# Hybrid mLSTM / stick-breaking layer: k projected ahead of q in the first set of heads, and all its heads turned by VectorE and transfers

## The chip, the cores and the metric

The kernel runs on one core of one Trainium2 chip. The metric is the device time of one execution in microseconds (us); lower is better. A core has a matrix engine (TensorE, PE in the profile, with its weight loads listed as PEld), a vector engine (VectorE, DVE), a scalar engine (ScalarE, ACT) and GpSimd (POOL). Transfers are issued from the queue of an engine; most of this kernel's are issued from SyncE (SP). Each engine works through its own instructions in the order in which the program issued them, and waits for the others by semaphores.

## The reference

One layer over x of 512 tokens by 1024 channels, all in float32. After an RMS norm, one input projection `w_in` gives the inputs of two token mixers and of the merge gates. Mixer A is an mLSTM with 4 heads of width 256. Mixer B, where the change lies, is stick-breaking attention with 8 heads of width 128:

```python
qs = rmsnorm(to_heads(sq, SB_HEADS), sb_q_norm_w)
ks_ = rmsnorm(to_heads(sk, SB_HEADS), sb_k_norm_w)
...
    z = jnp.einsum('bhtd,bhsd->bhts', qb, kb).astype(jnp.float32) * scale
...
    log_beta = jax.nn.log_sigmoid(z)
    log_1mb = jnp.where(causal, jax.nn.log_sigmoid(-z), 0.0)
    between = lax.cumsum(log_1mb, axis=3, reverse=True) - log_1mb
    a = jnp.where(causal, jnp.exp(log_beta + between), 0.0)
    outs.append(jnp.einsum('bhts,bhsd->bhtd', a.astype(v.dtype), vb))
```

Both mixers' outputs are gated, projected, merged by sigmoid gates and projected once more, and x is added.

## The kernel before

**Products in three parts.** To keep float32 accuracy every operand is split into a high half (a copy on ACT in a format that PE multiplies fast, `split` at L96, L97) and a low half (the difference, on DVE, L98), and each product is three matmuls: high by high, high by low, low by high (`mm3`, L91 to L94; the second of the three reads the low half of the moving operand). The split of a weight block writes `wh` and `wl`.

**Units.** All dense work is a list `units` of 512 KB weight blocks. A unit is 24 matmuls of 512 columns. The list is in the order of L862 to L1136. With the first set of four attention heads (`sets[0]`) it begins: four units for q (0 to 3), four for k (4 to 7), four for v (8 to 11), four for the gate z (12 to 15); then the second set's q (16 to 19), k (20 to 23) and so on. q, k and v are token groups: their four units go through the contraction, and each unit adds to all four PSUM banks (`dps`, four in all), one for each block of 128 tokens; they are evacuated together after the fourth unit. The very first group is different (`first`, L164): there each unit is one block of 128 tokens, so that the blocks are evacuated one by one, after units 0, 1, 2 and 3. z is a channel group: each unit fills one bank, evacuated a step later (L348, L350).

**The main loop** (L1263) makes one pass, here called a step, for each unit c. In this order it issues: the evacuation of unit c-1; the functions that are due at c (`later`, filled by `defer(n, fn)` with n steps of delay); the splits of units up to c+2 and loads further ahead (`ahead`); the first half of unit c's matmuls; one stage of each attention or mLSTM head in progress (`act`; in the steps of `REST`, among them 11 and 16, none moves on); the first stage of a head that starts now (`pend`, with `SB_START` at L27); the second half of unit c's matmuls.

**q and k of a head.** `qk_group` (L355) adds the bias to each token block (L364), squares and sums on ACT (L373), and takes the power -1/2 on POOL (L274, L275; for q a negative copy follows, L378). k is scaled by that on DVE a step later (L386); q isn't, its factor is applied in the sigmoids (L478, L482). Attention needs q and k with channels on partitions, so raw q and k must be turned. There are two ways. Either PE transposes the four blocks of a head through an identity into a PSUM bank (L455), when the head starts. Or `turn` (L399) does it for two heads at a time: four DVE transposes of 32 by 32 blocks (L405); a step later 16 transfers that put the blocks in place (`move`, L408 to L415), into a tile `tz`; for q, two more steps later, a DVE scaling with the norm weights (`weight`, L417 to L419). `TURNED` (L30) lists what takes the second way, as (name, set, pair of heads); in the first set all of q and the second pair of k. For k of the first pair PE does it.

**A head** (`head`, L444) is a generator. Its first stage splits the turned q and k into `qtt` and `ktt`. The next two hold the scores (L470), the sigmoids on ACT, the masks on POOL, the scan along the keys on DVE (L486) and products (L487), and DVE transposes of the weights (L504). Later stages move those blocks by transfers (L522) and multiply with v.

**The order before around the change.** q is evacuated in steps 1 to 4 and turned at steps 5 and 7 (moves at 6 and 8, weightings at 8 and 10). k is evacuated at step 8, scaled at 9 and 10, and its second pair turned at 11 with the move at 12. Heads 0, 1, 2, 3 start at steps 10, 13, 16, 20; heads 0 and 1 with four PE transposes each. All 16 transfers of a move go on SP's queue in the first set; in the second set every other one goes on POOL's (L414).

Of the kernel before, what the change touches and what calls it, by code (L numbers as in the profile page):

```python
# [17 lines left out]
TB = 4  # L18
# [3 lines left out]
C_SQ, C_SK, C_SV, C_SZ, C_GM, C_GS = 5128, 6152, 7176, 8200, 9224, 10248  # L22
# [1 line left out]

SB_START = [10, 13, 16, 20, 26, 28, 32, 34]  # L27
M_START = [52, 56, 70, 76]
GATES_PREP, GATES_START, GATES_SCAN = 2, 4, 35
TURNED = {("q", 0, 0), ("q", 0, 1), ("q", 1, 0), ("q", 1, 1), ("k", 0, 1), ("k", 1, 1)}  # L30
REST = {11, 16, 20, 23, 24, 32, 44, 64}
AHEAD, LOADS = 2, 4

# [2 lines left out]
def tile_hybrid_layer(  # L36
# [16 lines left out]
    nc = tc.nc  # L53
# [21 lines left out]
    def blk(tag, dt=F32, shape=(512,), name=None, p=128):  # L75

        where = mp if tag in MISC else sp
        return where.tile([p] + list(shape), dt, name=name or tag, tag=tag, bufs=BUFS[tag])

    def two(tag, dt=F32, name=None):  # L80

        t = blk(tag, dt, (2, 512), name=name)
        return t[:, 0, :], t[:, 1, :]

    def dense_ps():
        return psd.tile([128, 512], F32, name="dps", tag="dps")
# [4 lines left out]
    def mm3(ps, ah, al, bh, bl, first, last):  # L91
        nc.tensor.matmul(ps, ah, bh, start=first, stop=False)  # L92
        nc.tensor.matmul(ps, ah, bl, start=False, stop=False)  # L93
        nc.tensor.matmul(ps, al, bh, start=False, stop=last)  # L94
# [53 lines left out]
    def tok_group(src, c0, sta, evac, first=False, b0=None, row=None):  # L148
        ps = [None] * TB
        n0 = len(units)  # L150

        def evacs(ps):
            rest = None
            for tb in range(TB):
                then = evac(tb, ps[tb])
                if rest:
                    rest()
                rest = then
            if rest:
                rest()  # L160

        if row is not None:
            later.setdefault(n0 + (0 if first else 2), []).append(lambda: row.append(bias_row(b0)))
        if first:  # L164
            for tb in range(TB):
                u = Unit(src, c0, 256 * tb)
                u.evac = lambda tb=tb: evac(tb, f_ps[tb])
                units.append(u)
            return
        for g in range(4):  # L170
            u = Unit(src, c0, 256 * g)

            def mm(half, u=u, g=g):
                for tb in (2 * half, 2 * half + 1):
                    if g == 0:
                        ps[tb] = dense_ps()
                    for i in range(2):
                        k = 2 * g + i
                        sh, sl = sta(k, tb)
                        mm3(ps[tb], sh, sl, u.wh[:, i, :], u.wl[:, i, :], k == 0, k == KT - 1)  # L180

            u.mm = mm
            u.heavy = g == 3
            u.evac = (lambda: evacs(ps)) if g == 3 else (lambda: None)
            units.append(u)
# [11 lines left out]
    def defer(n, fn):  # L197
        later.setdefault(now[0] + n, []).append(fn)
# [74 lines left out]
    def rstd(dst, ssq, n, eps):  # L273
        nc.gpsimd.tensor_scalar(dst, ssq, 1.0 / n, eps, op0=OP.mult, op1=OP.add)  # L274
        nc.gpsimd.tensor_tensor(dst, dst, mhalf[:, 0:dst.shape[1]], op=OP.pow)  # L275
# [50 lines left out]
    def bias_row(c0):  # L326
        b = blk("brow")
        nc.sync.dma_start(b, bass.AP(tensor=b_in.tensor, offset=b_in.offset + c0, ap=[[0, 128], [1, 512]]))
        return b
# [6 lines left out]
    class SbSet:  # L336
# [18 lines left out]
        def qk_group(self, name, c0):  # L355
            row = []

            half = []

            def evac(tb, ps):  # L360
                if tb % 2 == 0:
                    half.extend(two("qk", name=name + "raw"))
                t = half[tb]
                nc.vector.tensor_tensor(t, ps, row[0], op=OP.add)  # L364
                self.raw[name].append(t)

                def norm():
                    ssq = tiny.tile([128, 4], F32, name="ssq", bufs=2)
                    rr = tiny.tile([128, 8], F32, name="r" + name, bufs=8 if name == "q" else 4)
                    r = rr[:, 0:4]  # L370
                    junk = blk("acc", BF, (128,), name="sqj")
                    for h in range(4):
                        nc.scalar.activation(junk, t[:, h * 128:(h + 1) * 128], AF.Square,  # L373
                                             accum_out=ssq[:, h:h + 1])
                    rstd(r, ssq, 128, EPS)
                    if name == "q":
                        rn = rr[:, 4:8]
                        nc.gpsimd.tensor_scalar(rn, r, -1.0, None, op0=OP.mult)  # L378
                        self.r.append((r, rn))
                        if tb == TB - 1:  # L380
                            defer(1, lambda: self.turn(name, 0))
                    else:
                        def scale():
                            for h in range(4):
                                hs = slice(h * 128, (h + 1) * 128)
                                nc.vector.tensor_scalar(t[:, hs], t[:, hs], r[:, h:h + 1], None, op0=OP.mult)  # L386
                            if tb == TB - 1:
                                done.add(("k", self.s))
                                defer(1, lambda: self.turn(name, 1))
                        defer(1, scale)  # L390

                if tb < 2 or name == "q" and self.s == 0:
                    norm()
                else:
                    defer(1, norm)

            tok_group(w_in, c0 + 512 * self.s, h_sta, evac, name == "q" and self.s == 0, c0 + 512 * self.s, row)

        def turn(self, name, g):  # L399

            ty = sp.tile([128, 8, TB, 32], F32, name="ty", tag="A", bufs=4)
            for tb in range(TB):
                nc.vector.transpose(ty[:, :, tb, :],  # L405
                                    self.raw[name][tb][:, 256 * g:256 * g + 256].rearrange("p (x j) -> p x j", j=32))

            def move():  # L408
                tz = blk("qk", F32, (2, 4, 128), name="tz")
                self.tz[name, g] = tz  # L410
                src = ty.rearrange("p (h b) i j -> p b h (i j)", h=2)
                for b in range(4):
                    for a in range(4):
                        q = nc.gpsimd if self.s and a % 2 else nc.sync  # L414
                        q.dma_start(tz[32 * b:32 * b + 32, :, a, :], src[32 * a:32 * a + 32, b])  # L415

            def weight():  # L417
                z = self.tz[name, g]
                nc.vector.tensor_scalar(z, z, qkw, None, op0=OP.mult)  # L419

            defer(1, move)
            if name == "q":
                defer(3, weight)
            if name == "q" and g == 0:
                defer(2, lambda: self.turn(name, 1))
# [18 lines left out]
        def head(self, h):  # L444
            hs = slice(h * 128, (h + 1) * 128)
            tr = []
            for name in ("q", "k"):
                th, tl = own = two("qk", FR, name=name + "tt")
                if (name, self.s, h // 2) in TURNED:
                    tp = self.tz[name, h // 2][:, h % 2].rearrange("p a (i j) -> p i a j", j=32)  # L450
                    th, tl = [x.rearrange("p (i a j) -> p i a j", a=4, j=32) for x in own]
                else:
                    tp = att_ps()
                    for tb in range(TB):
                        nc.tensor.transpose(tp[:, tb * 128:(tb + 1) * 128], self.raw[name][tb][:, hs], ident)  # L455
                if name == "q" and not (name, self.s, h // 2) in TURNED:
                    nc.scalar.activation(th, tp, AF.Copy, scale=qkw)
# [403 lines left out]

    sets = [SbSet(0), SbSet(1)]  # L862
    pairs = [MPair(0), MPair(1)]
    sets[0].qk_group("q", C_SQ)
    sets[0].qk_group("k", C_SK)
    sets[0].v_group()
    sets[0].z_group()
    sets[1].qk_group("q", C_SQ)
# [362 lines left out]
    for s in (0, 1):  # L1231
        for h in range(4):
            pend.append((SB_START[4 * s + h], 1,
                         lambda s=s: ("k", s) in done, lambda s=s, h=h: sets[s].head(h)))
# [102 lines left out]
```

## Time and profile before

| | us |
|---|---|
| median of 3 runs | 689.77 |
| range of the 3 runs | 689.24 to 689.87 |
| the profiled execution, whole | 689.49 |
| its span, from the first to the last instruction | 687.8 |
| PE busy in it | 681.0 |
| DVE busy | 467.2 |
| ACT busy | 337.1 |
| POOL busy | 111.7 |

The profile is of one execution. A row of its timeline has the start and the length in us, the engine, the line of the kernel, the operation, what it writes and reads, and how often; in brackets the idle time of the engine before it and what ended that. PE's matmuls overlap, so their rows last longer than the distance between their starts, and it is the starts that tell how fast PE goes. A row of the waits has who waited, for whom, us in total, times, and the longest.

### The profile page before, as it was taken

How to read it: one execution, taken by the hardware profiler on the slowest of the kernel's cores; microseconds unless marked ns; L12 is line 12 of the kernel's file. 1: busy time of each engine (PE TensorE's matmuls, PEld its weight loads, DVE VectorE, ACT ScalarE, POOL GpSimd, SP SyncE). 2: the span in 40 equal slices, each digit the busy share in tenths (PEclk: the TensorE clock that was granted, in tenths of full speed). 3: DMA queues.
4: the chain of work that ended last, by engine and by line, in shares of the span. 5: the costliest groups of instructions: out<-in, count | busy, mean ns of one | idle time of the engine just before them, and what ended most of it. 6: DMA issues, size and time to landing. Idle time of an engine off the chain costs nothing.

```text
span 687.8 us, 9389 instructions
## 1 busy us (share of the span) xinstructions
PE 681.0 (99%) x3162; PEld 568.9 (83%) x3162; DVE 467.2 (68%) x819; ACT 337.1 (49%) x631; POOL 111.7 (16%) x266
## 2 busy tenths in 40 slices
PE   8999999999999999999999999999999999999997
PEld 5888888888888888888888888888888888888876
DVE  6746787777997886789834648994352364445997
ACT  6245465566455653344466533448554343344451
POOL 4122042365430310000001210000112000111020
PEclk9999999999999999999999999999999999999999
DMA  7433543435463533643341343434223456599333
GB/s 250 139 95 107 160 138 105 134 112 149 134 171 86 124 111 83 139 95 92 107 117 53 107 109 85 128 91 134 68 64 90 115 176 200 141 206 205 121 82 103
DMA packets 122289, 84.74 MB, mean 123 GB/s; under 512 B 19018, under 2 KB 105956, under 8 KB 122240
## 3 DMA queue, kind: packets, MB, share of 16 engines
q1 hardware_dynamic: 119600, 77.97, 40.3%
q0 software_dynamic: 2496, 6.03, 4.7%
q8 instruction: 25, 0.41, 0.2%
q14 instruction: 24, 0.20, 0.1%
q10 hardware_dynamic: 144, 0.13, 0.1%
HBM read 66.22 MB, written 2.15 MB: 99 GB/s over the span
## 4 chain that ended last, share of the span: by engine, by line
PE 98%; DVE 1%; DMA 1%; SPq 0%; issue 0%; ACT 0%
PE dps L92 28%; PE dps L93 27%; PE dps L94 27%; PE aps L93 3%; PE aps L94 3%; PE aps L92 3%; PE dps L1216 1%; PE dps L1217 1%; PE dps L1218 1%; PE aps L811 1%; PE aps L813 1%; PE aps L812 1%; DMA stg<-in_w_in_dram 1%; PE aps L305 0%; DVE hl L317 0%; PE aps L591 0%
## 5 line engine op out<-in xcount | busy, mean ns | idle before, releaser
L98 DVE TENSOR_TENSOR wl<-stg,wh 128x1024 fp32r<-128x1024 f32 x92 | 112.5, 1223 | 106.0 <-ACT wh L97 105.5
L92 PE MATMUL dps<-hh,wh 128*128 128x512 f32 x448 | 175.0, 391 | 0.0
L94 PE MATMUL dps<-hh,wl 128*128 128x512 f32 x448 | 174.4, 389 | 0.0
L93 PE MATMUL dps<-hl,wh 128*128 128x512 f32 x448 | 174.4, 389 | 0.0
L97 ACT ACTIVATE wh<-stg 128x1024 fp32r<-128x1024 f32 x92 | 96.8, 1052 | 64.5 <-PE dps L94 44.3
L94 PEld LDWEIGHTS dps<-hh,wl 128*128 128x128 f32 x448 | 84.1, 188 | 17.7
L93 PEld LDWEIGHTS dps<-hl,wh 128*128 128x128 f32 x448 | 84.2, 188 | 16.8
L92 PEld LDWEIGHTS dps<-hh,wh 128*128 128x128 f32 x448 | 84.1, 188 | 16.7
L92 PE MATMUL dps<-wh,hh 128*128 128x512 f32 x224 | 87.7, 392 | 0.0
L94 PE MATMUL dps<-wh,hl 128*128 128x512 f32 x224 | 87.3, 390 | 0.0
L93 PE MATMUL dps<-wl,hh 128*128 128x512 f32 x224 | 87.2, 389 | 0.0
L94 PEld LDWEIGHTS dps<-wh,hl 128*128 128x128 f32 x224 | 42.0, 188 | 9.0
L92 PEld LDWEIGHTS dps<-wh,hh 128*128 128x128 f32 x224 | 42.1, 188 | 8.3
L93 PEld LDWEIGHTS dps<-wl,hh 128*128 128x128 f32 x224 | 42.1, 188 | 8.2
L704 DVE SCALAR_TENSOR_TENSOR acc<-tmp,vec,acc 128x511 f32<-128x511 f32 (+2 forms) x48 | 36.0, 750 | 1.7
L707 ACT ACTIVATE tmp<-acc 128x512 f32<-128x512 f32 x16 | 10.1, 633 | 50.8 <-DVE acc L704 50.8
L480 POOL TENSOR_SCALAR_AFFINE_SELECT om<-om 128x128 f32<-128x128 f32 x32 | 15.3, 479 | 96.2 <-ACT om L478 96.1
L486 DVE TENSOR_TENSOR_SCAN om<-om 128x512 f32<-128x512 f32 (+3 forms) x32 | 26.7, 834 | 5.5 <-POOL om L480 5.5
L764 POOL TENSOR_SCALAR_AFFINE_SELECT w_all<-om 128x128 f32<-128x128 f32 x16 | 5.3, 363 | 144.4 <-DMA om<-rb_d 144.4
L478 ACT ACTIVATE om<-aps,rq 128x512 f32<-128x512 f32 (+3 forms) x32 | 16.8, 524 | 21.0 <-PE aps L94 21.0
L94 PE MATMUL dps<-yh,wl 128*128 128x512 f32 x64 | 24.9, 389 | 0.0
L92 PE MATMUL dps<-yh,wh 128*128 128x512 f32 x64 | 24.9, 389 | 0.0
(249 smaller groups left out, 1217.8 us busy)
## 6 DMA issues: line engine op xcount, KB each, us to landing
stg<-in_w_in_dram SPq DMA_DIRECT2D x87, 512.0 KB, 3.9
az<-ay SPq DMA_DIRECT2D x128, 40.0 KB, 2.9
stg<-in_w_proj_s_dram SPq DMA_DIRECT2D x8, 512.0 KB, 4.7
B<-in_w_out_dram SPq DMA_DIRECT2D x8, 512.0 KB, 6.6
stg<-in_w_proj_m_dram SPq DMA_DIRECT2D x8, 512.0 KB, 5.9
wl<-stg POOLq DMA_DIRECT2D x8, 512.0 KB, 5.9
tz<-ty SPq DMA_DIRECT2D x72, 32.0 KB, 1.9
brow<-in_b_in_dram SPq DMA_DIRECT2D x8, 256.0 KB, 4.5
```

The source lines that it names most:

```text
L92: nc.tensor.matmul(ps, ah, bh, start=first, stop=False)
L93: nc.tensor.matmul(ps, ah, bl, start=False, stop=False)
L94: nc.tensor.matmul(ps, al, bh, start=False, stop=last)
L97: nc.scalar.activation(hi, src, AF.Copy)
L98: nc.vector.tensor_tensor(lo, src, hi.bitcast(F32), op=OP.subtract)
L478: nc.scalar.activation(om[:, 0:n], zp, AF.Sigmoid, scale=rn[:, h:h + 1])
L480: nc.gpsimd.affine_select(out=om[:, ts], in_=om[:, ts], compare_op=OP.is_gt, fill=1.0, base=0, channel_multiplier=1, pattern=[[-1, 128]])
L486: nc.vector.tensor_tensor_scan(back, back, back, 1.0, op0=OP.mult, op1=OP.bypass)
L704: nc.vector.scalar_tensor_tensor(acc[:, j:], t[:, 0:T - j], cw(3 - j, ch), acc[:, j:], op0=OP.mult, op1=OP.add)
L707: nc.scalar.activation(t, acc, AF.Sigmoid)
L811: nc.tensor.matmul(nm[:, 0:258], ph, vh, start=j == 0, stop=False)
L812: nc.tensor.matmul(sum_v, ph, vl, start=False, stop=False)
```

## The change

Line numbers of the kernel before apply. In the first set:

- k's group is issued ahead of q's, so k takes the place of the first group (units 0 to 3, block by block) and q that of the second (units 4 to 7, evacuated together).
- k's first pair joins `TURNED`: heads 0 and 1 no longer have PE transposes. k's scale is due a step after each evacuation (steps 2 to 5); its first pair is turned at step 6, its second at 7, with moves at 7 and 8.
- q is turned at the end of its evacuation: the first pair at step 8 (move at 9, weighting at 11), the second at step 10 (move at 11, weighting at 13).
- In the second set q's first turn is due at the same step as before, only put down at another place.
- The moves of the first set send every other transfer on POOL's queue, as those of the second set do.
- Head 0 starts at step 11 rather than 10, head 2 at 15 rather than 16. Steps 11 and 16 are in `REST`, so the stages after the first stay in the steps that they had.

```diff
-SB_START = [10, 13, 16, 20, 26, 28, 32, 34]
+SB_START = [11, 13, 15, 20, 26, 28, 32, 34]
...
-TURNED = {("q", 0, 0), ("q", 0, 1), ("q", 1, 0), ("q", 1, 1), ("k", 0, 1), ("k", 1, 1)}
+TURNED = {("q", 0, 0), ("q", 0, 1), ("q", 1, 0), ("q", 1, 1), ("k", 0, 0), ("k", 0, 1), ("k", 1, 1)}
...
                         self.r.append((r, rn))
-                        if tb == TB - 1:
-                            defer(1, lambda: self.turn(name, 0))
                     else:
...
                             if tb == TB - 1:
                                 done.add(("k", self.s))
-                                defer(1, lambda: self.turn(name, 1))
+                                if self.s == 0:
+                                    defer(1, lambda: self.turn(name, 0))
+                                defer(2 - self.s, lambda: self.turn(name, 1))
                         defer(1, scale)
 
-                if tb < 2 or name == "q" and self.s == 0:
+                if name == "q" and tb == TB - 1:
+
+                    if self.s:
+                        defer(2, lambda: self.turn(name, 0))
+                    else:
+                        self.turn(name, 0)
+                if tb < 2 or name == "k" and self.s == 0:
                     norm()
                 else:
                     defer(1, norm)
 
-            tok_group(w_in, c0 + 512 * self.s, h_sta, evac, name == "q" and self.s == 0, c0 + 512 * self.s, row)
+            tok_group(w_in, c0 + 512 * self.s, h_sta, evac, name == "k" and self.s == 0, c0 + 512 * self.s, row)
...
-                        q = nc.gpsimd if self.s and a % 2 else nc.sync
+                        q = nc.gpsimd if a % 2 else nc.sync
...
+    sets[0].qk_group("k", C_SK)
     sets[0].qk_group("q", C_SQ)
-    sets[0].qk_group("k", C_SK)
```

## The prediction

> **What bounds the kernel now.** I read the page first: its first two parts and the chain that ended last.
>
> ```profile
> span 687.8 us, 9389 instructions
> PE 681.0 (99%) x3162; PEld 568.9 (83%) x3162; DVE 467.2 (68%) x819; ACT 337.1 (49%) x631; POOL 111.7 (16%) x266
> PEclk9999999999999999999999999999999999999999
> PE 98%; DVE 1%; DMA 1%; SPq 0%; issue 0%; ACT 0%
> ```
>
> TensorE (PE) is busy for 99% of the span at full granted clock, and 98% of the chain that sets the end is its own work. Next I asked who PE waits for:
>
> ```profile
> PE dps L1184 <- DVE idle L1179: 1.5, 1, 1.5
> PE dps L1216 <- DVE hh L309: 1.0, 1, 1.0
> PE aps L305 <- DVE x L297: 0.8, 2, 0.6
> ```
>
> That is the whole list: 3.3 us, all before 14 us. Later PE never waits. So two things alone can move the end: PE instructions that go away, and a new wait on PE. A relieved queue or engine is worth nothing by itself.
>
> **What is removed.** "Unit n" is the n-th weight block, "step n" the pass of the main loop that issues its matmuls. The PE timeline shows the transposes of raw k for head 0 (in unit 10) between ordinary matmuls, and the starts of units 10, 11 and 12:
>
> ```profile
> 71.25 0.39 PE L92 MATMUL dps<-wh,hh 128*128 128x512 f32 x1
> 73.74 0.39 PE L94 MATMUL dps<-wh,hl 128*128 128x512 f32 x1
> 73.97 0.60 PE L455 MATMUL aps<-ident,kraw 128*128 128x128 f32 x4
> 74.33 0.48 PE L92 MATMUL dps<-wh,hh 128*128 128x512 f32 x1
> 74.64 0.40 PE L93 MATMUL dps<-wl,hh 128*128 128x512 f32 x1
> 77.18 0.39 PE L92 MATMUL dps<-wh,hh 128*128 128x512 f32 x1
> 82.62 0.39 PE L92 MATMUL dps<-hh,wh 128*128 128x512 f32 x1
> ```
>
> Unit 11 has no head work and lasts 82.62 - 77.18 = 5.44 us; unit 10 lasts 77.18 - 71.25 = 5.93. Four transposes cost 0.49 us. The change drops two such groups, heads 0 and 1 (step 13): **-0.98 us**, 0.14% of the span, and nothing else leaves PE.
>
> **What is added where there is room.** Turning k for heads 0 and 1 costs VectorE (DVE) four transposes at step 6; scaling k moves from steps 9 and 10 into steps 2 to 5; the first q turn moves to step 8, in place of a weighting.
>
> ```profile
> 50.78 1.23 DVE L98 TENSOR_TENSOR wl<-stg,wh 128x1024 fp32r<-128x1024 f32 x1 [4.21 <-ACT wh L97]
> 51.92 1.42 DVE L405 STREAM_TRANSPOSE ty<-qraw 128x256 f32<-128x256 f32 x4
> 63.76 1.65 DVE L386 TENSOR_SCALAR kraw<-kraw,rk 128x128 f32<-128x128 f32 x8
> ```
>
> The turn is 1.42 us in a hole of 4.21 us. The scales are 0.83 us a block; what they push back is weight splits that PE uses some 8 us after they end (the one at 50.78, done by 52.0, is unit 8's, which starts two ordinary units ahead of unit 10: 71.25 - 2 x 5.44 = 60.4). I cost both at 0; without that cover they would cost their own 0.2 to 1.4 us. Half of the moves leave SP for GpSimd (POOL). SP issues 8 rather than 16 for a move, and weight loads behind them start earlier; since PE waits for no load, 0.
>
> **Where a new wait comes.** Head 0's split of q and k (two ACT copies, two DVE subtractions) moves from step 10 to 11, and the weightings of q move from steps 8 and 10 to 11 and 13. Here is DVE around it, with the copy on ACT that releases it:
>
> ```profile
> 77.38 1.06 ACT L97 ACTIVATE wh<-stg 128x1024 fp32r<-128x1024 f32 x1 [2.17 <-PE dps L94]
> 78.47 1.23 DVE L98 TENSOR_TENSOR wl<-stg,wh 128x1024 fp32r<-128x1024 f32 x1 [1.21 <-ACT wh L97]
> 79.62 1.28 DVE L433 TENSOR_TENSOR tmp<-dps,brow 128x512 f32<-128x512 f32 x2
> 85.53 1.23 DVE L98 TENSOR_TENSOR wl<-stg,wh 128x1024 fp32r<-128x1024 f32 x1 [0.26 <-ACT wh L97]
> 87.90 1.22 DVE L486 TENSOR_TENSOR_SCAN om<-om 128x512 f32<-128x512 f32 x1 [1.14 <-POOL om L480]
> 90.77 0.74 DVE L350 SCALAR_TENSOR_TENSOR ys<-dps,bvec,tmp 128x512 f32<-128x512 f32 x1
> 96.27 0.68 DVE L98 TENSOR_TENSOR qtt<-tz,qtt 128x512 fp32r<-128x512 f32 x1
> 96.88 0.68 DVE L98 TENSOR_TENSOR ktt<-aps,ktt 128x512 fp32r<-128x512 f32 x1
> ```
>
> At step 11 DVE can't run ahead: unit 13's weight split (78.47) waits for ACT's copy, and that for PE to leave unit 10. PE leaves 0.49 earlier, so the split starts at 77.98. Behind it now stand head 0's two subtractions, one per 0.61 us (96.27 to 96.88): +1.22. The bias adds of v, at 79.62 so far, start at 79.62 - 0.49 + 1.22 = 80.35, **0.73 late**. From there the work is a chain: adds and low halves back to back until the weight split at 85.53, ACT's high halves between them, then ACT's next weight copy, sigmoids, POOL's masks, the scan at 87.90. Each waits for the one before, so the 0.73 lasts through the hole of 1.14 us. At step 13 the second weighting of q (L419) joins the queue ahead of the rest. Its price:
>
> ```profile
> 68.69 0.75 DVE L419 TENSOR_SCALAR tz<-tz,qkw 128x1024 f32<-128x1024 f32 x1 [0.37 <-DMA tz<-ty]
> 69.36 0.87 DVE L386 TENSOR_SCALAR kraw<-kraw,rk 128x128 f32<-128x128 f32 x4
> ```
>
> 0.67 us from start to start. Between 90.77 and 96.88 the timeline marks no idle time of DVE, so head 1's k low half, 96.88 + 0.68 = 97.56 so far, ends at 97.56 + 0.73 + 0.67 = 98.96. Who waits for it? PE, at head 1's scores in step 14:
>
> ```profile
> 98.63 0.39 PE L92 MATMUL aps<-ktt,qtt 128*128 128x512 f32 x1
> 98.86 0.39 PE L93 MATMUL aps<-ktt,qtt 128*128 128x512 f32 x1
> 12.47 0.74 DVE L297 TENSOR_SCALAR x<-x,xs 128x1024 f32<-128x1024 f32 x1
> 13.28 1.09 PE L305 MATMUL aps<-ident,x 128*128 128x128 f32 x8 [0.16 <-DVE x L297]
> ```
>
> The second matmul reads that low half. It had 98.86 - 97.56 = 1.30 us to spare. With 0.98 us of PE work gone it wants to start at 97.88. DVE's end reaches PE in 0.07 us (12.47 + 0.74 = 13.21, start 13.28), so it starts at 99.03: **+1.15 us**. After an interruption the next start comes 0.31 instead of 0.23 later (74.33 to 74.64): about +0.1. All later PE work is queued behind that matmul.
>
> Bounds of this wait: 0, if something in the chain of step 12 takes up the lag; 1.15 as worked out; more, if step 11 starts later (the rival below). I take 1.15, since each term has its own row.
>
> Head 1 keeps its step. Head 2's split moves from step 16 to 15, ahead of unit 15's evacuation, whose bank PE takes for unit 16's fourth token block:
>
> ```profile
> 109.67 0.75 DVE L350 SCALAR_TENSOR_TENSOR ys<-dps,bvec,tmp 128x512 f32<-128x512 f32 x1
> 108.75 0.39 PE L92 MATMUL dps<-wh,hh 128*128 128x512 f32 x1
> ```
>
> Two subtractions (1.22) and up to 0.6 of lag that remains put its end near 110.4 + 1.8 = 112.2; the bank is wanted at 108.75 + 0.27 + 18 x 0.227 = 113.1. Cost 0, with 0.9 to spare.
>
> **POOL.** The moves put eight issues each on POOL's queue:
>
> ```profile
> L415 POOL DMA_DIRECT2D tz<-ty x24: 533/533/795, 151.9 to 188.7; - x24
> DMA to landing us min/median/max: 1.8/3.2/5.0
> 59.93 0.19 POOL L274 TENSOR_SCALAR rk<-ssq 128x4 f32<-128x4 f32 x1 [18.61 <-ACT sqj L373]
> 39.69 0.19 POOL L274 TENSOR_SCALAR rq<-ssq 128x4 f32<-128x4 f32 x1 [0.17 <-ACT sqj L373]
> 41.09 0.23 POOL L378 TENSOR_SCALAR rq<-rq 128x4 f32<-128x4 f32 x1
> 169.16 4.39 POOL L415 DMA_DIRECT2D tz<-ty  x8
> 172.06 1.69 DVE L386 TENSOR_SCALAR kraw<-kraw,rk 128x128 f32<-128x128 f32 x8
> ```
>
> A block's norm takes POOL 41.32 - 39.69 = 1.6 us, up to 2.0 beside DVE; a move's eight issues 4.4. At steps 8 and 9 POOL's queue becomes: two norms from 59.93 to about 63.9, k's second move to 68.4, a norm to 70.1, q's first move to 74.6, a norm. The last issue, at 74.1, lands 1.8 to 5.0 later: 75.9 to 79.1, by the median 77.3. The weighting of q at step 11 (0.75) is behind it, and head 0's copies on ACT want it done by 77.95 (unit 13's copy ends then). At the median it ends at 78.05: no real delay. The norms only have to be there for the sigmoids, some 10 us later: 0.
>
> [...]
>
> **The sum.** -0.98 + 1.15 + 0.1 = +0.27 us. The profiled execution took 689.49 us (687.8 of span, 1.7 around it); it would become 689.76. The median of the runs shown, 689.77, lies 0.28 above that execution; on it the forecast is 690.04, rounded to **690.0 us**: what PE saves it waits for two units later. About 0.2% (1.4 us) is what a measurement of this kernel can tell from no change.
>
> **Rivals.**
> 1. *The saving stays.* The wait at step 14 doesn't come or is a part of what I worked out: 689.77 - 0.98 = 688.8, or up to 689.6 with half the wait. For it: DVE is only 68% busy, and the margin was 1.30. Against: from step 11 each link has a row. Chance 0.25. More than 0.98 can't be gained, as PE has no other wait to lose.
> 2. *POOL is late* (the slower side). If q's first move lands after 77.2, the weighting holds unit 13's split and head 0's copies, and each us goes on down the same chain to the wait at step 14: +0.27 + (landing - 77.2). At the largest landing, 79.1, that is +2.2: 692.0. It decides "slower" from a landing of 78.3, where the total is +1.4. For it: two moves and four norms stand in one queue. Against: the median lands in time. Chance 0.2 for a delay that shows, half of it over the bound.
> 3. *POOL's issues are starved.* If DVE work stretched each issue, both moves ahead of the weighting would grow. By the worst row, 0.795 for each, it is 16 x 0.26 = 4.2 us at step 11, which puts the landing 4.3 past 77.2 and the time at 690.0 + 4.3 = 694.3. Against: DVE's fp32 scaling at 172.06 ran beside the eight issues from 169.16, which took 4.39 us together, 0.55 each. Chance 0.05. [...]
>
> **How the numbers follow.** Forecast 0.5 (689.6 to 690.5), rival 1 0.25, rival 2 0.2, rival 3 0.05. The range 688.8 to 691.6 takes in rival 1 whole and rival 2 to a landing of 78.5. Faster by over 0.2% needs 1.4 us, over what leaves PE: 0.04. Slower: half of rival 2 and rival 3, 0.14. Same: 0.82.
>
> **What would show it.** Eight L455 transposes instead of sixteen, the first in set 1. PE's waits get a fourth row, scores (aps L93) waiting for DVE's ktt at L98, about 1.2 us in unit 14. DVE's adds of v start near 80.35. Wrong would be: no PE wait after 14 us (rival 1); the weighting at step 11 marked as waiting for tz (rival 2); eight POOL issues well above 4.5 us (rival 3).

## The result and the profile after: 695.06 us, ratio 1.007

| | before | after |
|---|---|---|
| median of 6 runs, us | 689.85 | 695.06 |
| range of the 6 runs | 689.24 to 690.5 | 692.13 to 695.92 |
| ratio to before, 95% interval | | 1.007, 1.0051 to 1.0089 |
| the profiled execution, whole | 689.49 | 695.92 |
| its span | 687.8 | 694.1 |

The change makes the kernel slower by 5.2 us. (One run among all that follow, of the kernel early_56, took 1391.78 us and is counted in no median.) The forecast was 690.0 within 688.8 to 691.6; the time lies above that range, on the side of the rival "POOL is late". The first lines of the page of the changed kernel, and its chain by engine:

```profile
span 694.1 us, 9414 instructions
...
PE 682.4 (98%) x3154; PEld 569.4 (82%) x3154; DVE 468.1 (67%) x823; ACT 336.9 (49%) x631; POOL 130.0 (19%) x298
...
PE 91%; issue 3%; DMA 2%; POOL 2%; DVE 1%; ACT 0%; SPq 0%; DVEq 0%; POOLq 0%
```

PE has 8 instructions fewer, as foreseen (3154 for 3162), yet its share of the chain fell from 98% to 91%: it waits now. The waits of PE in the changed kernel (for whom, us in total, times, longest):

```profile
PE aps L93 <- DVE ktt L98: 2.0, 1, 2.0
PE dps L1222 <- ACT fh L1167: 1.5, 1, 1.5
PE dps L1190 <- DVE idle L1185: 1.5, 1, 1.5
PE dps L94 <- DMA wl<-stg: 1.2, 1, 1.2
PE dps L92 <- DVE tmp L439: 1.0, 1, 1.0
```

The second and third rows are the start, where the kernel before waits too. The first and the last are new and belong to the change; the fourth is new as well. To see what each costs I cut the span at the first matmul of four units, in the timeline of PE. Units 4 and 20 enclose every step that the change touches. Before:

```profile
38.61 0.39 PE L92 MATMUL dps<-wh,hh 128*128 128x512 f32 x1
...
132.46 0.40 PE L92 MATMUL dps<-wh,hh 128*128 128x512 f32 x1
```

and after:

```profile
39.95 0.39 PE L92 MATMUL dps<-wh,hh 128*128 128x512 f32 x1
...
136.40 0.39 PE L92 MATMUL dps<-wh,hh 128*128 128x512 f32 x1
```

| stretch | before | after | difference |
|---|---|---|---|
| up to the start of unit 4 | 38.61 | 39.95 | +1.34 |
| unit 4 to unit 20, "the middle" below | 93.85 | 96.45 | +2.60 |
| unit 20 to unit 103 | 507.55 | 507.52 | 0 |
| unit 103 to unit 106 | 27.62 | 29.17 | +1.55 |
| unit 106 to the end of the span | 20.2 | 21.0 | +0.8 |

**The middle.** Nearly all of the 2.60 is explained by one chain. Here are the rows of POOL's two moves at steps 8 and 9, and of DVE behind them, in the changed kernel:

```profile
65.22 4.31 POOL L421 DMA_DIRECT2D tz<-ty  x8
71.56 4.36 POOL L421 DMA_DIRECT2D tz<-ty  x8 [0.33 <-issue]
```

```profile
80.83 0.75 DVE L425 TENSOR_SCALAR tz<-tz,qkw 128x1024 f32<-128x1024 f32 x1 [5.73 <-DMA tz<-ty]
81.50 1.22 DVE L98 TENSOR_TENSOR wl<-stg,wh 128x1024 fp32r<-128x1024 f32 x1
82.64 0.68 DVE L98 TENSOR_TENSOR qtt<-tz,qtt 128x512 fp32r<-128x512 f32 x1
83.24 0.69 DVE L98 TENSOR_TENSOR ktt<-tz,ktt 128x512 fp32r<-128x512 f32 x1
83.84 1.28 DVE L439 TENSOR_TENSOR tmp<-dps,brow 128x512 f32<-128x512 f32 x2
...
95.80 0.74 DVE L425 TENSOR_SCALAR tz<-tz,qkw 128x1024 f32<-128x1024 f32 x1
...
101.92 0.69 DVE L98 TENSOR_TENSOR ktt<-tz,ktt 128x512 fp32r<-128x512 f32 x1
```

The first weighting (L425, step 11) leaves DVE idle for 5.73 us because of q's first move, and unit 13's split, head 0's two subtractions and v's bias adds (L439) follow it without a gap. The view of that move's eight transfers on POOL has first the length of an issue (ns, smallest, median, largest) and then the time from issue to landing:

```profile
L421 POOL DMA_DIRECT2D tz<-ty x8: 533/534/609, 71.6 to 75.4; - x8
DMA to landing us min/median/max: 4.7/5.0/5.6
```

The last of the eight is issued at 75.39 and lands 4.8 us later, at 80.17; the weighting starts 0.66 us after that. Two instructions of PE are held up at the end of this chain, again in the changed kernel:

```profile
84.68 0.47 PE L92 MATMUL dps<-hh,wh 128*128 128x512 f32 x1 [1.05 <-DVE tmp L439]
...
102.66 0.50 PE L93 MATMUL aps<-ktt,qtt 128*128 128x512 f32 x1 [1.96 <-DVE ktt L98]
```

The first is unit 12, which needs a bank that v's adds free. The second is head 1's scores, where the prediction had put the wait. The waits are 1.05 + 1.96; each also breaks the pipeline, about 0.26 each by the starts; 0.98 of transposes is gone: 3.01 + 0.52 - 0.98 = 2.55, against 2.60 measured.

**The last store.** The view of the transfers gives the median time from issue to landing. The store that ends the kernel, before:

```profile
out_dram<-xr ACTq DMA_DIRECT2D x1, 128.0 KB, 1.9
```

and after:

```profile
out_dram<-xr ACTq DMA_DIRECT2D x1, 128.0 KB, 2.8
```

This is the 0.8 at the end. The other two differences, at the start and in unit 103, needed more executions to be judged.

### The profile page after: what moved, and what is told of

It reads as the page before. It is cut to its first block, busy times and chain, and to the rows that moved or that the text cites. A ratio compares the mean times of both kernels' runs of the same rounds, so it can differ in the third digit from the quotient of the medians.

```text
span 694.1 us, 9414 instructions
## 1 busy us (share of the span) xinstructions
PE 682.4 (98%) x3154; PEld 569.4 (82%) x3154; DVE 468.1 (67%) x823; ACT 336.9 (49%) x631; POOL 130.0 (19%) x298
## 3 DMA queue, kind: packets, MB, share of 16 engines
HBM read 66.22 MB, written 2.15 MB: 99 GB/s over the span
## 4 chain that ended last, share of the span: by engine, by line
PE 91%; issue 3%; DMA 2%; POOL 2%; DVE 1%; ACT 0%; SPq 0%; DVEq 0%; POOLq 0%
PE dps L92 25%; PE dps L94 25%; PE dps L93 25%; PE aps L93 3%; PE aps L94 3%; PE aps L92 3%; DMA wl<-stg 1%; POOL tz L421 1%; PE dps L1222 1%; PE dps L1223 1%; PE dps L1224 1%; DMA stg<-in_w_in_dram 1%; PE aps L817 1%; PE aps L819 1%; PE aps L818 1%
## 5 line engine op out<-in xcount | busy, mean ns | idle before, releaser
L770 POOL TENSOR_SCALAR_AFFINE_SELECT w_all<-om 128x128 f32<-128x128 f32 x16 | 6.9, 464 | 142.5 <-DMA om<-rb_d 128.0
L421 POOL DMA_DIRECT2D tz<-ty x56 | 30.9, 558 | 9.7 <-DVE ty L411 8.9
L486 POOL TENSOR_SCALAR_AFFINE_SELECT om<-om 128x128 f32<-128x128 f32 x32 | 14.3, 447 | 85.3 <-ACT om L484 85.2
```

Of the source, the lines that this page charges most:

```text
L486: nc.gpsimd.affine_select(out=om[:, ts], in_=om[:, ts], compare_op=OP.is_gt, fill=1.0, base=0, channel_multiplier=1, pattern=[[-1, 128]])
```

## The experiments

Ten kernels: before_pool edits the kernel before, early_56 edits early_head, the others the changed kernel. "Middle" is from unit 4 to unit 20 in the profiled execution, "lowered clock" whether the granted clock fell in it. In the texts that were written before each run letters stand for theories here and there; the paragraph around each says in words which theory is at stake.

| kernel | middle | lowered clock | last store | median (runs) | ratio to before |
|---|---|---|---|---|---|
| before | 93.85 | no | 1.9 | 689.85 (6) | |
| after | 96.45 | no | 2.8 | 695.06 (6) | 1.007, 1.0051 to 1.0089 |
| again | 97.65 | yes | 2.8 | 694.68 (6) | 1.0071, 1.0054 to 1.0088 |
| k1_on_sp | 94.17 | no | 2.0 | 690.56 (12) | 1.0009, 0.9998 to 1.002 |
| weight_on_k | 93.51 | no | 2.8 | 690.83 (12) | 1.0021, 1.0007 to 1.0035 |
| columns_swapped | 97.48 | yes | 2.8 | 693.76 (6) | 1.0052, 1.0037 to 1.0067 |
| transposes_back | 95.80 | no | 2.8 | 692.62 (9) | 1.0038, 1.0025 to 1.005 |
| fill_the_wait | 96.36 | no | 2.9 | 693.06 (6) | 1.0045, 1.003 to 1.0061 |
| before_pool | 93.85 | no | 1.9 | 690.24 (12) | 1.0006, 0.9995 to 1.0017 |
| early_head | 92.97 | no | 1.9 | 689.03 (12) | 0.9987, 0.9977 to 0.9998 |
| early_56 | 92.96 | no | 2.9 | 695.5 (4) | 1.0084, 1.007 to 1.0098 |
| k0_on_sp | 97.51 | yes | 1.9 | 693.18 (5) | 1.0058, 1.0044 to 1.0071 |

### The same kernel again

The changed kernel with no edit, to tell what belongs to it from what belongs to one execution.

> The changed kernel once more, for a second trace. The loss was 6.3 us of span: 1.34 ahead of unit 4 (first weights later, granted clock dips to 0.64), 2.60 between the starts of units 4 and 20 (96.45 us against 93.85), 2.36 behind. Theory A: the middle part belongs to the schedule and comes again to 0.3 us (96.2 to 96.8), with waits of about 1.0 us before unit 12 and 2.0 us on ktt; the other two are chance of transfers and differ this time by up to 2 us. Rival: all three belong to the schedule and come again alike.

The start of unit 4 fell back to 38.92 and the wait in unit 103 is not in its list; both were matters of one execution. Elsewhere the start was late in kernels of either kind (39.92 in before_pool, 40.43 in columns_swapped). But the middle took 97.65, over the 96.2 to 96.8 that I had expected, and something new appeared. The windows of this execution (us, then the busy time of PE, PEld, DVE, ACT and POOL, the granted clock, DMA share, GB/s):

```profile
98.00:101.00 3.00, 1.32 (x6) 0.75 (x4) 2.83 (x5) 0.05 (x1) 0.00 (x0) 1.00 0.40 146
101.00:104.00 3.00, 2.73 (x9) 2.44 (x10) 3.00 (x9) 1.45 (x3) 0.43 (x2) 0.54 0.00 0
104.00:107.00 3.00, 3.00 (x13) 2.48 (x12) 2.63 (x5) 0.44 (x2) 1.56 (x5) 0.89 0.70 216
```

and PE's rows in them:

```profile
101.28 0.80 PE L93 MATMUL aps<-ktt,qtt 128*128 128x512 f32 x1 [1.96 <-DVE ktt L98]
101.87 0.63 PE L94 MATMUL aps<-ktt,qtt 128*128 128x512 f32 x1
...
103.58 0.63 PE L92 MATMUL dps<-hh,wh 128*128 128x512 f32 x1
104.00 0.63 PE L93 MATMUL dps<-hl,wh 128*128 128x512 f32 x1
```

Behind the same wait of 1.96 us the granted clock is 0.54, and matmuls of 512 columns start 0.43 us apart (103.58 to 104.00 to 104.43) instead of 0.23. Here the wait costs a second time, after it has ended; in the first execution of the changed kernel the same wait of 1.96 us had left the clock at 1.00. That was in no term of mine, and became a theory to test.

### POOL's queue: k's second move back on SP

```diff
-                        q = nc.gpsimd if a % 2 else nc.sync
+                        q = nc.gpsimd if a % 2 and (self.s, name, g) != (0, "k", 1) else nc.sync
```

> The second move of k is issued on SP alone, so POOL's queue has two norms and a norm ahead of q's first move instead of two norms, eight issues and a norm. Theory A (the late landing of q's first move, behind POOL's queue, sets the waits): the first weighting of q runs some 2 to 4 us earlier, at 76 to 78.5; the wait before unit 12 goes, the one on ktt falls from 2.0 to about 1.1; units 4 to 20 take 94.2 to 94.7 us, the time falls by about 2 us. Rival B (the waits come from DVE's order alone, wherever the move lands): 96.4 us, no change.

The rows of POOL, DVE and PE in this kernel, with the landing of the eight transfers behind the first:

```profile
65.83 4.33 POOL L421 DMA_DIRECT2D tz<-ty  x8 [0.33 <-PE dps L94]
DMA to landing us min/median/max: 1.7/1.8/2.3
```

```profile
73.28 0.77 DVE L425 TENSOR_SCALAR tz<-tz,qkw 128x1024 f32<-128x1024 f32 x1
```

```profile
98.64 0.50 PE L93 MATMUL aps<-ktt,qtt 128*128 128x512 f32 x1 [0.97 <-DVE ktt L98]
```

With one move out of POOL's queue, q's first move is issued from 65.83 on instead of 71.56 and has landed when DVE is free for the weighting, which no longer waits. The wait before unit 12 is gone and that for ktt is 0.97. The middle is +0.32 against before, where my sum without a late POOL was +0.27. This one edit takes back 4.5 of the 5.2 us, twice what I had expected: 2.3 in the middle and 0.8 at the last store; the rest isn't told apart by this run.

The move gained more than its place in the queue. Counted from the start of unit 4, its last landing comes 7.05 us earlier than in the changed kernel, 4.0 of them by the earlier issue and 3.0 because a transfer lands sooner there. What is issued later lands late in this kernel too: q's second move, from 72.18 on, takes 4.4 to 5.8 us from issue to landing, but its consumer isn't waiting yet.

### The weighting moved off q

The norm weights can be multiplied into k just as well, whose moves are earlier:

```diff
-            if name == "q":
+            if name == ("q" if self.s else "k"):
                 defer(3, weight)
```

> In the first set the norm weights are applied to the turned k (steps 9 and 10) instead of the turned q (11 and 13); the product is the same. q's move is as late as in the changed kernel. Theory A: at step 11 ACT's copies of q wait for the landing instead of DVE, 0.8 us sooner as no weighting stands between; at step 13 DVE saves 0.67. The wait before unit 12 falls to about 0.2, the one on ktt by 0.7 more; units 4 to 20 take about 95.0 us, the time falls by 1.5. Rival C (POOL's lateness alone counts, the weightings nothing): 96.0 to 96.5 us.

PE's wait at head 1's scores, in this kernel:

```profile
PE aps L93 <- DVE ktt L98: 0.3, 1, 0.3
```

The middle is 93.51, below that of before, where I had expected about 95.0: without the two weightings in steps 11 and 13 most of the wait is gone. POOL still issues as late (q's first move from 70.96 to 75.6), but the move had landed, at 77.41, in time for head 0's split at 78.46: its last transfer took 2.4 us where it took 4.8 in the changed kernel. SP's loads of weights and a bias row stand just ahead of the move in both (69.18 to 71.22 in the changed kernel, 68.44 to 70.49 here), but SP's eight issues of q's second move began at 73.17 instead of 71.35. So contention with SP's move may have a part in the long landing; that is argued, not shown. The median, 690.83, still lies 0.9 over the 689.96 of before in the same series; the last store lands 0.9 later than there.

### The columns exchanged

q takes k's columns of the weights and of the bias, and k those of q, so that the order of the loads is that of the kernel before; the output is then not that of the layer.

```diff
-    sets[0].qk_group("k", C_SK)
-    sets[0].qk_group("q", C_SQ)
+    sets[0].qk_group("k", C_SQ)
+    sets[0].qk_group("q", C_SK)
```

> The changed kernel with the columns of q and k in w_in exchanged in the first set (k's group reads q's columns and bias, q's group k's), so the output differs; the schedule is the same. It tests the first 40 us. Theory D (where the first block lies in memory decides when it lands): unit 4 starts near 38.6 us, the granted clock stays at 1.0 in the first 20 us, and the time falls by about 1.3 us. Rival E (chance from execution to execution, or the schedule): unit 4 starts anywhere from 38.6 to 40, and the median is that of the changed kernel to 0.5 us.

Unit 4 started at 40.43, later than in any other run, so it isn't the columns that delayed the start. The middle has the wait and the lowered clock of again (0.79 and 0.64 in 101 to 107). The theory of the columns fell.

### The clock: dummy work in the wait, and the transposes put back

If a wait of PE lowers its clock, work that fills the wait must make the kernel faster. Eight matmuls of 512 columns, into a bank that the scores overwrite next, ahead of head 1's scores:

```diff
             z3, z01 = att_ps(), att_ps()
+            if (self.s, h) == (0, 1):
+                for _ in range(8):
+                    nc.tensor.matmul(z3, qh[:, 384:512], kh, start=True, stop=True)
```

> Eight more matmuls of high halves are issued ahead of head 1's scores, into the bank that the scores then start afresh (1.8 us of PE, all inside a wait of 2.0 us plus the pipeline). In two of three traces PE went at half pace for about 3 us behind the wait on ktt (starts 0.43 instead of 0.23 us apart), 1.0 to 1.2 us more. Theory G (the granted clock falls because PE stood idle): no such stretch, units 4 to 20 take 96.3 to 96.7 us, the median falls by 0.5 to 1.2 us from about 694.7. Rival H (the stretch has another cause): it is seen as often, 97.5 us in most traces, and the median stays or grows.

The same windows in this kernel (columns as before):

```profile
101.00:104.00 3.00, 2.88 (x16) 2.17 (x15) 3.00 (x7) 1.33 (x3) 0.36 (x1) 1.00 0.01 3
104.00:107.00 3.00, 3.00 (x15) 2.47 (x14) 2.79 (x8) 1.33 (x4) 1.86 (x5) 1.00 0.68 204
```

The clock stays at 1.00. The median is 693.06 and all six runs lie within 692.63 to 693.73, where those of again went from 693.14 to 697.18 (median 694.68). The difference of 1.6 us is more than the 0.5 to 1.2 expected, and since the intervals of the two ratios overlap its size is rough; the profiled executions give the same (the last table below). That much of the loss came from the clock after the wait, not from the wait.

The other test gives PE work back that the change had removed, in the first set k's first pair is transposed by PE as before; its turn and its moves stay:

```diff
-TURNED = {..., ("k", 0, 0), ("k", 0, 1), ("k", 1, 1)}
+TURNED = {..., ("k", 0, 1), ("k", 1, 1)}
```

> The changed kernel with head 0's and head 1's k turned by PE again (eight transposes, 0.98 us of PE); the turn and moves of k's first pair still run, unused. Theory A (PE waits for a chain that starts at the landing of q's first move, so that the saving is swallowed): the waits before unit 12 and on ktt shrink by about 0.5 us each and units 4 to 20 take 96.2 to 96.7 us as in the changed kernel without a clock dip (96.45); no change of the time. Rival F (the saving is there, and the waits come on top): 97.4 us, the time 1.0 us longer than the changed kernel's.

The wait for head 1's scores and the weighting, in this kernel:

```profile
PE aps L93 <- DVE ktt L98: 1.5, 1, 1.5
```

```profile
78.82 0.76 DVE L425 TENSOR_SCALAR tz<-tz,qkw 128x1024 f32<-128x1024 f32 x1 [5.06 <-DMA tz<-ty]
```

Four transposes, 0.49, fill a part of the wait, which is 1.5 now; the clock isn't lowered, and the nine runs lie within 691.97 to 693.1. 0.98 us of work more on PE made the kernel 2.1 us faster than again, where I had expected no change and a middle of 96.2 to 96.7. The two middles differ by 1.85: 0.25 since the weighting started earlier, counted from the start of unit 4, and the rest, as far as the last table goes, by the clock.

### POOL's issues in the kernel before

```diff
-                        q = nc.gpsimd if self.s and a % 2 else nc.sync
+                        q = nc.gpsimd if a % 2 else nc.sync
```

> The kernel before with one edit: in the first set every other transfer of a move goes on POOL's queue. Theory A (POOL's queue hurts only where a move is due a step before it is needed): here the weightings of q come two steps after the moves and head 0 another step or two later; no new wait, units 4 to 20 take 93.8 to 94.0 us, no change of the time. Rival J (POOL's transfers themselves disturb): over 94.3 us.

The middle is 93.85, to the digit that of before, and the interval of the ratio holds 1. The issues on POOL cost nothing by themselves: DVE's second weighting does wait 2.1 us for them there, but nothing that PE needs comes late by it. They cost when a consumer stands right behind them (2.3 us of the middle, by k1_on_sp).

### A version that keeps the saving

The two edits of k1_on_sp and weight_on_k together, and head 0 back at step 10, so that its split no longer stands in step 11:

```diff
-SB_START = [11, 13, 15, 20, 26, 28, 32, 34]
+SB_START = [10, 13, 15, 20, 26, 28, 32, 34]
```

> Three edits of the changed kernel together: the norm weights on k in the first set, k's second move on SP alone, head 0 started at step 10 again. Theory A: nothing stands behind unit 13's split, the lag of 0.73 and the weighting's 0.67 are gone, q's first move lands in time, no wait is left on ktt or before unit 12; units 4 to 20 take 92.8 to 93.0 us, the whole 0.98 is kept, and the time is 0.7 to 1.0 us under the kernel before, as far as the first loads allow. Rival I (head 0's split now waits at step 10 for the landing and holds ACT and DVE there): a wait stays, 93.3 to 94.5 us.

Its waits of PE:

```profile
PE dps L1222 <- DVE hh L309: 1.8, 1, 1.8
PE dps L1190 <- DVE idle L1185: 1.5, 1, 1.5
PE aps L305 <- DVE x L297: 0.7, 2, 0.5
```

Nothing after the start. The middle is 92.97, 0.88 below before: the transposes' 0.98 is there when nothing is late behind it. The median is 689.03 to before's 689.71 in the same series, ratio 0.9987 with an interval of 0.9977 to 0.9998: a gain, but at the edge of what can be told.

### The last store, and POOL's part again

The store's landing followed the number of the moves' issues on POOL: 1.9 or 2.0 with 24 or 48, 2.8 or 2.9 with 56. Two kernels test this from both sides. early_56 is early_head with the second set's move of k's second pair wholly on POOL; k0_on_sp is the changed kernel with k's first move wholly on SP.

```diff
+                        q = nc.gpsimd if (a % 2 and (self.s, name, g) != (0, "k", 1)) or (self.s, name, g) == (1, "k", 1) else nc.sync
...
+                        q = nc.gpsimd if a % 2 and (self.s, name, g) != (0, "k", 0) else nc.sync
```

> early_head with one more move all on POOL, so that POOL issues 56 of the moves instead of 48; q's first move of set 0 is as early as there. Theory that the count of POOL's issues sets how late the last store lands: its landing is 2.8 us instead of 1.9, units 4 to 20 still take 92.9 to 93.1 us, and the median is about 0.9 us over early_head's 689.0, so 689.9. Rival, that the late store came with the late landing of set 0's q or from something else: landing 1.9, median 689.0 within 0.4.

> The changed kernel with k's first move of set 0 wholly on SP, so 48 issues on POOL; q's first move is issued by POOL at the same step as before, but with nothing ahead of it in POOL's queue. Theory that q's lateness comes from POOL's queue being occupied by k's moves as well as from the late issue: q0 is issued from its split at once, as in the changed kernel (there POOL waited only 0.33 us), so it lands as late, 80 to 81 us; units 4 to 20 take 96.4 us, or 97.5 with a stretch at a lowered clock. If the count of POOL's issues sets the last store, its landing is 1.9 and the median about 0.85 us under the changed kernel's 694.7, so 693.8; if not, landing 2.8 and 694.7.

The transfers of early_56:

```profile
tz<-ty POOLq DMA_DIRECT2D x56, 32.0 KB, 3.2
...
out_dram<-xr ACTq DMA_DIRECT2D x1, 128.0 KB, 2.9
```

and of k0_on_sp:

```profile
tz<-ty POOLq DMA_DIRECT2D x48, 32.0 KB, 3.7
...
out_dram<-xr ACTq DMA_DIRECT2D x1, 128.0 KB, 1.9
```

The store goes with the count in both, in one kernel without the late move and in the other with it. Why 56 differs from 48, some 500 us after the last of these issues (192.6 in the changed kernel), stays open.

The time of early_56 was missed by far: 695.5 for an expected 689.9. My edit had made a fault of the same kind in another place. Its POOL, DVE and PE:

```profile
184.48 7.94 POOL L421 DMA_DIRECT2D tz<-ty  x15
193.05 0.54 POOL L421 DMA_DIRECT2D tz<-ty  x1 [0.64 <-DMA tz<-ty]
...
193.62 0.31 POOL L486 TENSOR_SCALAR_AFFINE_SELECT om<-om 128x128 f32<-128x128 f32 x1
```

```profile
193.97 0.81 DVE L492 TENSOR_TENSOR_SCAN om<-om 128x256 f32<-128x256 f32 x1 [4.33 <-POOL om L486]
```

```profile
198.18 0.50 PE L93 MATMUL aps<-ktt,qtt 128*128 128x512 f32 x1 [3.53 <-DVE ktt L98]
```

Sixteen issues in a row keep a head's mask (L486) from its turn, the scan waits 4.33 us for it, the next head's ktt is behind the scan, and PE waits 3.53 us; the granted clock then is 0.65 and 0.78 in the two windows of 3 us from 199 on. From the start of unit 20 to that of unit 39 it takes 131.14 instead of 125.7, +5.4; with 0.9 for the store, 689.0 + 6.3 = 695.3.

In k0_on_sp my text was wrong to say that nothing stands ahead of q's move: k's second move still does (POOL 63.92 to 68.42, then a norm, then q's from 70.44). The weighting started at 80.48, as late as expected; PE waited 2.0 ahead of unit 12, which lowered the clock there (0.53 in 85 to 88), and then only 0.4 for ktt. The store is at 1.9, and the median of 693.18 is 0.6 under the 693.8 expected for that case.

## Why the prediction was wrong, point by point

- **The removed work** was right: eight L455 transposes less, 3154 instructions of PE for 3162, and early_head's middle is 0.88 below before's.
- **The new wait at head 1's scores** was right in place and size. Where POOL isn't late (k1_on_sp), the list has the fourth row that I asked for, 1.0 us where I said about 1.2, and the middle is +0.32 where I had +0.27. v's adds start there at 80.33, counted from the start of unit 4 in the kernel before, where I had 80.35.
- **The room for turns, scales and loads** held: PE waits for none of them. Head 2 at step 15 cost nothing: PE has no wait there in any run.
- **POOL's issue times** were right: 4.31 and 4.36 for the eight issues of each of the two moves (4.2 to 4.8 for any eight in this kernel), so nothing is starved, and rival 3 fell. The order in POOL's queue was right too; a norm took 1.6 us there (61.28 to 62.91), the one beside DVE's split of a weight block 2.2 (63.06 to 65.27). Read against the kernel before (1.34 earlier, the difference at the start), the issues of q's move end at 74.6 in both the forecast and the trace.
- **The step that failed is the landing of q's first move, and what follows it.** I took the median of a row, 3.2 us after the last issue, and let the weighting start at once: "at the median it ends at 78.05: no real delay". Counted from the start of unit 4 in the kernel before, the last issue starts at 74.05, where I had 74.1. It takes 4.8 us to land, not 3.2, and lands at 78.83, inside the 75.9 to 79.1 of the forecast but far from the 77.3 that I chose. The weighting starts another 0.66 us after that, at 79.49; that step I had put at nothing. The row was of transfers of the second set; these ran beside SP's eight issues of q's second move (71.35 to 77.30) and SP's loads (issued at 70.85 and 77.40). k's second move one step earlier (65.22 on) took 1.7 to 1.9 us from issue to landing, less than half of the 4.7 to 5.6 of q's.
- **The rival's price was right, if the start of the weighting is put for the landing.** It said +0.27 + (landing - 77.2); with the landing at 78.83 it gives +1.90, with the start of the weighting +2.56, for the 2.60 measured. The starts below are counted from the start of unit 4 in the kernel before:

| kernel | start of the weighting, shifted | rival 2's price | middle minus before's | rest |
|---|---|---|---|---|
| transposes_back | 78.83 | 1.90 | 1.95 | 0.05 |
| columns_swapped | 78.96 | 2.03 | 3.63 | 1.60, lowered clock |
| again | 79.08 | 2.15 | 3.80 | 1.65, lowered clock |
| fill_the_wait | 79.39 | 2.46 | 2.51 | 0.05 |
| after | 79.49 | 2.56 | 2.60 | 0.04 |
| k0_on_sp | 80.45 | 3.52 | 3.66 | 0.14 |

  In six kernels the formula gives the middle to 0.15, but for 1.6 where the clock fell behind ktt. In k0_on_sp the clock fell ahead of ktt, and PE had to wait for ktt anyway: it cost nothing. In columns_swapped the profile puts the end of DVE's wait down to a weight load, though the weighting starts 0.67 after the move's last landing as in the others. So rival 2 was the case, and its chance of 0.2, half of it over the bound, the mistake: in every kernel that kept POOL's queue and the weighting of q, the weighting started between 78.8 and 80.5.
- **Two more terms were missing.** They are the clock behind a wait of about 2 us (1.6 us, by fill_the_wait against again), and the last store (0.8 to 0.9; 0.85 is taken here). Together: 689.85 + 2.6 + 0.85 = 693.3, with 1.6 more where the clock falls, 694.9; the median is 695.06. That the clock fell behind this wait in the runs of the median is argued, not shown: in the profiled execution, at 695.92, it didn't, and the start and unit 103 made up the time; two of the other five runs, at a mean clock of 1.0, took 692.13 and 695.6. The range's upper end, 691.6, is by the rival's formula a landing of 78.8, not the 78.5 named beside it. It fell short because it had no term for the 0.66, the clock and the store.

## What to carry to other kernels

A transfer whose consumer has no slack should be judged by the slowest landing that the trace shows, not by the median, and by what passes between the landing and the consumer's start, above all when its issues stand behind others in the same queue: moving eight of k's issues away took 4.5 us off the median here, 2.3 of them in the middle, while the same issues cost nothing where nobody waits. A wait of PE of about 2 us may be charged twice, once for itself and once for the clock after it (1.96 us and 1.6 more in again); and work taken from a saturated engine counts only if what it waits for next comes that much earlier too (early_head keeps 0.88 of the 0.98).

## What the runs showed of the hardware

- **The clock falls after short waits.** In the middle, a wait of 1.0 or 1.5 us (k1_on_sp, transposes_back) left the clock at 1.00; 1.9 to 2.0 us lowered it in again (0.54), columns_swapped (0.79 and 0.64) and k0_on_sp (0.53), not in the profiled execution of after; 3.5 us did in early_56 (0.65 and 0.78). Matmuls of 512 columns then start 0.43 us apart instead of 0.23 for about 3 us (101.28 to 104.43 in again), in windows of 3 us with a granted clock of 0.54 and 0.89. So 1.9 to 2.0 us were enough in three executions of four; what sets the fourth apart isn't shown. At the start the same fall came in some executions and not in others, in the changed kernel (0.64) and in before_pool (0.63) alike:

```profile
9.00:12.00 3.00, 2.43 (x6) 1.94 (x7) 2.93 (x10) 2.76 (x6) 2.71 (x4) 0.64 1.04 399
```

  where the kernel before has

```profile
9.00:12.00 3.00, 2.82 (x12) 2.29 (x13) 2.93 (x11) 2.69 (x6) 2.83 (x4) 1.00 1.05 415
```

- **From issue to landing** transfers of one size differ by a factor of three within one kernel: the eight on POOL of k's second move took 1.7 to 1.9 us in the changed kernel (65.22 on), those of q's first 4.7 to 5.6 us (71.56 on). That SP's loads and moves beside them are the reason is argued, not shown.
- **From landing to use.** Wherever a weighting waited for transfers of POOL, it started 0.66 to 0.68 us after the last of them had landed (eight waits in eight kernels; q's first move in six, q's second in before_pool, k's second in weight_on_k). The one that waited for SP's, in the kernel before (68.69), started 0.27 us after. Why is open.
- **The last store** lands in 1.9 to 2.0 us with 24 or 48 of the moves' issues on POOL and in 2.8 to 2.9 with 56, in all twelve kernels. The cause is open.
- Open as well: what part SP's concurrent move and its loads have in the 5 us landing, and what made one weight transfer late in unit 103 of one execution.
